# Where six weight casts stand in ScalarE's order at the start of a two-mixer decoder layer

## The chip, the cores and the metric

One core of a Trainium2 chip runs one launch of the whole layer. The metric is the device time of that launch in microseconds (us), the median of three runs.

## The reference

One post-norm layer on 1024 tokens of width 1024, batch 1, all in float32:

```
h    = layer_norm(x)
proj = h @ w_in                                   # 1024 x 11296
u, b_gate, c_gate, z_a, z_s, xbc, dt_raw, g_a, g_s = split(proj)
y_a  = (silu(z_a) * b_gate * conv3(c_gate * u)) @ w_a_out
xs, bs, cs = split(silu(conv4(xbc) + bias))
dt   = softplus(dt_raw + dt_bias)
y_s  = ssd_chunked(xs, dt, -exp(a_log), bs, cs) + xs * d_skip     # chunks of 128 tokens
y_s  = grouped_rmsnorm(y_s * silu(z_s)) @ w_s_out
out  = (sigmoid(g_a) * y_a + sigmoid(g_s) * y_s) @ w_o
h    = layer_norm(alpha * h + out)
```

## The kernel before, in words

Matrix products run in three float32r passes: a weight is split into a head (a cast, tile `whip`) and a rest (the weight minus its head, tile `wlop`), the activations likewise, and head x head, head x rest and rest x head are added up in PSUM. Heads of weights are cast by ScalarE (`prep_hi`), rests are subtracted by VectorE (`prep_lo`).

The input projection takes 44 pairs of column tiles. Each pair runs as seven Strassen-Winograd products of 512-token, 512-row pieces (`PROD`: which weight combination meets which activation combination). A product of a pair is an item: 12 matmuls of 128x128 by 128x512. The first three pairs (`EARLY = 3`) are worked through together, product by product in the order 1, 2, 3, 6, 5, 7, 4, so items 0 to 20 are "early" and item 21 (`START`) is where the steady part begins. Items 0 to 2 are product 1 (`a11` with `b11`, into `pU`), items 3 to 5 product 2 (`a12` with `b21`), items 6 to 8 product 3, whose weight `s4` GpSimd makes from `a12` and other sums.

Product 1 and 2 need only the first 512 tokens; product 3 needs the second 512 (`b22`), and products 6, 5, 7, 4 need sums over quarters of the normalised activations (`quarter_sums`, tiles `t`). The start of the program is therefore:

- the first half of the layer norm (`x0` to `x3`), eight transposed tiles, their evacuation by ScalarE (`evac`, `hf0...`), and the heads and rests of `b11` and `b21` by VectorE;
- statistics and norms of the second half (`factors(4)`, `norm(4)`, ..., `norm(6)`; `x4` to `x7`), on VectorE and ScalarE;
- items 0 to 5, then `dt_project(0)` (the projection `dps0` of the step sizes), then `second_half()`: 32 transposes in three PSUM banks, their evacuations, and between them the heads of items 6, 7 and 8.

For this early part a scheduler orders each engine's instructions by what it expects to be ready, except for instructions issued through `q(engine, f)`: these stand on their engine in the order in which the code issues them. The layer norm, the evacuations and the transposes of the first half, and GpSimd's sums go through `q`; matmuls, rests of weights and the additions from PSUM (`oa`) don't. GpSimd's `s4` of pair 0 also waits for the norm of `x7` on VectorE, and GpSimd's eight later sums stand behind it. From item 21 on the order is the written one.

In the code, all heads of the early pairs, items 0 to 20, go through `q` on ScalarE (item 0's is cast by VectorE). The loop over the items that asks for them is written behind the norms of the second half:

```
        if eng is None and kind == "p" and i < EARLY:
            q(S, lambda: S.activation(flat(hi), src, AF.Copy))
```

Of the kernel before, what the change touches and what calls it, by code (L numbers as in the profile page):

```python
# [45 lines left out]
def trunk_kernel(ctx: ExitStack, tc: tile.TileContext, x, w_in, w_dt, w_a, w_s, w_o, par, con,  # L46
# [60 lines left out]
    def flat(t):  # L107
        return t.rearrange("p k f -> p (k f)")
# [76 lines left out]
    EARLY = 3  # L185
# [19 lines left out]
    items += [("s", g, j) for g, j in s_order]  # L205
    item_at = {it: n for n, it in enumerate(items)}
    LA, LF = 3, 5

    raws, s1s, ops = {}, {}, {}

# [6 lines left out]
    def fetch(n):  # L217

        if n >= len(items) or items[n][:2] in raws or items[n] in raws:
            return  # L220
        kind, i, j = items[n]
        if kind == "p":
            for w in ("a11", "a12", "a21", "a22"):
                fetch_block(i, w)
        else:
            r = rawt(f"raw_{kind}{i}_{j}")
            SP.dma_start(r, w_a[i, :, j * HALF:(j + 1) * HALF] if kind == "a" else
                         w_s[4 * i + j // 2, :, j % 2 * HALF:(j % 2 + 1) * HALF])
            raws[items[n]] = r

    def combine(p):

        if p in s1s:
            return
        r = raws["p", p]
        s1, s2 = (est.tile([P, HALF], F32, name=f"e{n}_{p}") if p < 2 and n == "s1" else
                  r["a11"] if p < 2 else ap.tile([P, HALF], F32, tag=n, name=f"{n}_{p}") for n in ("s1", "s2"))
        fs = [lambda: Gp.tensor_tensor(s1, r["a21"], r["a22"], ALU.add),  # L238
              lambda: Gp.tensor_tensor(s2, s1, r["a11"], ALU.subtract),
              lambda: Gp.tensor_tensor(r["a21"], r["a11"], r["a21"], ALU.subtract)]  # L240
        if p < 2:
            fs = [fs[0], fs[2], fs[1]]
        for f in fs:
            q(Gp, f) if p < EARLY else f()
        s1s[p] = {"s1": s1, "s3": r["a21"], "s2": s2}

    def combine_last(p):

        if "s4" in s1s[p]:
            return  # L250
        a12 = raws["p", p]["a12"]
        f = lambda: Gp.tensor_tensor(a12, a12, s1s[p]["s2"], ALU.subtract)  # L252
        if p < EARLY:
            ins = q(Gp, f)
            if p == 0:
                tc.add_manual_dep(ins.ins, normed[0].name,
                                  mybir.DependencyInfo(mybir.DependencyClass.Sync, mybir.DependencyReason.DATA), reason="later")
        else:
            f()
        s1s[p]["s4"] = a12  # L260

    def source(n):
        kind, i, j = items[n]
        if kind != "p":
            return raws[items[n]]
        which = PROD[j][0]
        if which[0] == "s":
            combine(i)
            if which == "s4":
                combine_last(i)  # L270
            return s1s[i][which]
        return raws["p", i][which]
# [3 lines left out]
    def prep_hi(n, eng=None):  # L276

        if n >= len(items) or n in his:
            return
        fetch(n)  # L280
        src = source(n)
        kind, i, j = items[n]
        hi = his[n] = ap.tile([P, 4, P], F32R, tag="whi", name=f"whi{kind}{i}_{j}", bufs=LA + 1)
        if eng is None and kind == "p" and i < EARLY:
            q(S, lambda: S.activation(flat(hi), src, AF.Copy))
        elif eng is None:
            S.activation(flat(hi), src, AF.Copy)  # L287
        else:
            eng.tensor_copy(flat(hi), src)
# [10 lines left out]
    def prep(n, eng=None):  # L300
        prep_hi(n, eng)
        return prep_lo(n)
# [43 lines left out]
    def q(eng, f):  # L346

        if eng in last:
            with tc.issue_after(last[eng].ins):
                ins = f()  # L350
        else:
            ins = f()
        last[eng] = ins
        return ins
# [85 lines left out]
    def second_half():  # L440
        order = (4, 5, 6, 7, 0, 1, 2, 3)
        trs = {k: bank(("c4", "tr", "st")[i % 3], f"tr1{k}") for i, k in enumerate(order)}
        for k in order:
            for s in (4, 5, 7, 6):
                PE.transpose(trs[k][:, s % 4 * P:(s % 4 + 1) * P], xs[s][:, k * P:(k + 1) * P], ident)
            evac(1, k, trs[k])
            if k in (5, 7, 1):
                prep_hi(2 * EARLY + (5, 7, 1).index(k))
# [31 lines left out]
    def dt_turn():  # L480
        trd = bank("tr", "trd")
        trd3 = trd.rearrange("p (c h) -> p c h", c=NCH)
        for c in range(NCH):
            PE.transpose(trd3[:, c, :], dT[c // 4][:2 * H, c % 4 * P:(c % 4 + 1) * P], ident[:2 * H, :2 * H])
        w4.append(cv("w4").rearrange("p (i h c) -> p i h c", i=4, h=H))
        v = w4[0][:, 0]
        S.activation(v, trd3[:, :, 0:H].rearrange("p c h -> p h c"), AF.Copy)
        V.tensor_tensor(v, v, trd3[:, :, H:].rearrange("p c h -> p h c"), ALU.add)
        V.tensor_tensor(v, v, db_t.unsqueeze(2).to_broadcast([P, H, NCH]), ALU.add)
# [406 lines left out]
    def load_gy(j):  # L896
        M[j] = place(SG[j], f"sg{j}")
        SP.dma_start(M[j], sgs_d[j])
        gy[j] = otile(f"yg{j}", j % 2 if j < KT - 1 else 0)
        SP.dma_start(gy[j], yag_d[j])  # L900
# [159 lines left out]
    for n, it in enumerate(items):  # L1060
        if it[0] == "p" and it[2] == 1:
            first_of[n] = it[1]
    START = 7 * EARLY
    dt_work, first_cv = None, -1
    for n, (kind, i, j) in enumerate(items):
        now[0] = n
        for k in range(n, n + LF + 1):
            fetch(k)
        if n >= START and n + 2 in first_of:
            combine(first_of[n + 2])  # L1070
        if n >= START and n - 2 in first_of:
            combine_last(first_of[n - 2])
        if n < START:
            for k in range(n, min(n + LA + 1, 2 * EARLY if n < 2 * EARLY else START + LA)):
                prep_hi(k)
                if k < n + LA:
                    prep_lo(k)
        else:
            prep_hi(n + LA)
            prep_lo(n + LA - 1)  # L1080
        hi, lo = ops.pop(n)
        ops[n] = None
        if kind == "p":
# [6 lines left out]
            if n == 4 * EARLY + 1:  # L1090
                dt_project(1)
                dt_turn()
            if n == START - 1:
                est.release()
# [10 lines left out]
        if n in gy_at:  # L1105
            load_gy(gy_at[n])
        if n == START - 1:
            dt_work = dt_steps()
# [150 lines left out]
```

## Time and profile before

| | |
|---|---|
| median of three runs | 1420.25 us (1419.54, 1420.25, 1424.09) |
| the profiled execution | 1420.99 us, span of the core 1418.8 us |
| TensorE busy | 1383.5 us, 98% of the span |
| VectorE, ScalarE, GpSimd busy | 975.8, 701.4, 485.5 us |

The profile is of one execution. Its span runs from the first to the last instruction of the core; its own time holds 2.2 us besides. Times inside the profile are counted from the span's start. Items 0 to 20, on which the change acts, lie in the first 110 us or so.

### The profile page before, as it was taken

To read this page: it belongs to the slowest core of one execution; us is meant where nothing else is said; L and a number is where in the kernel's file an instruction comes from. 1 tells how busy PE (TensorE), PEld (TensorE's weight loads), DVE (VectorE), ACT (ScalarE), POOL (GpSimd) and SP (SyncE) were. 2 spreads that over 40 slices of the span, in tenths; PEclk is the share of its full clock that TensorE was granted. 3 is DMA by queue.
4 is the path that set the end of the run, shared out by engine and by line. 5 is a ranking of instruction groups with operands and counts; after the bars stand their busy time and mean duration, and the time that the engine had idled before them with its cause. 6 is when DMAs were issued, how large, how long until landed. Compare 5 with 4: busy or idle time off the path is not lost. (4 is left out here: it accounts for less than half of the span.)

```text
span 1418.8 us, 18394 instructions
## 1 busy us (share of the span) xinstructions
PE 1383.5 (98%) x6532; PEld 1111.4 (78%) x6532; DVE 975.8 (69%) x1422; ACT 701.4 (49%) x1228; POOL 485.5 (34%) x367
## 2 busy tenths in 40 slices
PE   6899999999999999999999999999999999999997
PEld 4677887888887888887888888888878888888786
DVE  7776878787779778688878686767464463224764
ACT  4465566555466655566566565555452231113421
POOL 1312124444425454334444343434230000000496
PEclk9899999999999999999999999999999999999999
DMA  6012354554444555444555654554547663223322
GB/s 237 15 67 83 118 134 130 126 182 127 145 125 132 144 165 151 131 130 123 156 156 182 134 153 127 153 126 127 186 163 267 232 228 133 90 82 118 127 89 89
DMA packets 166459, 198.09 MB, mean 140 GB/s; under 512 B 10688, under 2 KB 116064, under 8 KB 166368
## 3 DMA queue, kind: packets, MB, share of 16 engines
q1 hardware_dynamic: 158160, 167.14, 40.5%
q10 hardware_dynamic: 8208, 29.79, 5.3%
q8 instruction: 51, 0.84, 0.2%
q14 instruction: 40, 0.33, 0.1%
HBM read 146.28 MB, written 50.61 MB: 139 GB/s over the span
## 5 line engine op out<-in xcount | busy, mean ns | idle before, releaser
L105 DVE TENSOR_TENSOR wlop<-raw_a,whip 128x512 fp32r<-128x512 f32 x210 | 186.0, 886 | 158.7 <-ACT whip L287 63.9
L1015 PE MATMUL p<-b,whip 128*128 128x512 f32 x352 | 145.1, 412 | 7.2 <-DVE oa L1024 4.4
L1015 PE MATMUL pU<-t,whip 128*128 128x512 f32 x352 | 145.1, 413 | 0.0
L1015 PE MATMUL p<-t,whip 128*128 128x512 f32 x352 | 142.0, 403 | 0.0
L1016 PE MATMUL p<-b,whip 128*128 128x512 f32 x352 | 141.5, 402 | 0.0
L1017 PE MATMUL p<-b,wlop 128*128 128x512 f32 x352 | 140.8, 400 | 0.0
L1016 PE MATMUL pU<-t,whip 128*128 128x512 f32 x352 | 139.3, 396 | 0.0
L1017 PE MATMUL p<-t,wlop 128*128 128x512 f32 x352 | 139.1, 395 | 0.0
L1016 PE MATMUL p<-t,whip 128*128 128x512 f32 x352 | 139.1, 395 | 0.0
L1017 PE MATMUL pU<-t,wlop 128*128 128x512 f32 x352 | 139.0, 395 | 0.0
L675 POOL TENSOR_TENSOR xw<-xd,dte_t 128x256 f32<-128x256 f32 x56 | 46.9, 838 | 260.8 <-DVE xd L661 260.8
L287 ACT ACTIVATE whip<-raw_a 128x512 fp32r<-128x512 f32 x205 | 124.4, 621 | 22.4 <-issue 10.5
L940 POOL TENSOR_TENSOR res<-res,ag 128x1024 f32<-128x1024 f32 x8 | 19.7, 2462 | 276.1 <-ACT res L939 271.2
L238 POOL TENSOR_TENSOR s<-raw_a,raw_a 128x512 f32<-128x512 f32 x42 | 69.2, 1648 | 97.9 <-DVE wlop L105 85.8
L859 PE MATMUL p_ws<-y,whis 128*128 128x512 f32 x256 | 100.9, 394 | 0.0
L858 PE MATMUL p_ws<-y,whis 128*128 128x512 f32 x256 | 100.8, 394 | 0.0
L860 PE MATMUL p_ws<-y,wlos 128*128 128x512 f32 x256 | 100.7, 393 | 0.0
L105 DVE TENSOR_TENSOR wlos<-raw_s,whis 128x512 fp32r<-128x512 f32 x32 | 22.2, 693 | 113.0 <-PE p_ws L860 89.2
L252 POOL TENSOR_TENSOR raw_a<-raw_a,s 128x512 f32<-128x512 f32 x42 | 67.5, 1607 | 90.3 <-issue 78.8
L105 DVE TENSOR_TENSOR wlop<-s,whip 128x512 fp32r<-128x512 f32 x84 | 80.3, 966 | 13.4 <-PE p L1017 8.5
L1015 PEld LDWEIGHTS p<-b,whip 128*128 128x128 f32 x352 | 67.4, 192 | 23.7 <-issue 4.8
L641 ACT ACTIVATE em<-em,cum_t 128x128 f32<-128x128 f32 x256 | 81.3, 390 | 6.5 <-ACT ob L585 3.6
(224 smaller groups left out, 3345.7 us busy)
## 6 DMA issues: line engine op xcount, KB each, us to landing
raw_a<-in_w_in_dram SPq DMA_DIRECT2D x168, 256.0 KB, 3.9
em<-cum_d SPq DMA_DIRECT2D x64, 256.0 KB, 7.0
xg_d<-cv ACTq DMA_DIRECT2D x16, 512.0 KB, 6.4
xT<-xg_d SPq DMA_DIRECT2D x32, 256.0 KB, 4.6
z<-zs_d SPq DMA_DIRECT2D x32, 256.0 KB, 2.9
gat_d<-y SPq DMA_DIRECT2D x32, 256.0 KB, 2.9
gt<-gat_d SPq DMA_DIRECT2D x16, 512.0 KB, 6.7
raw_s<-in_w_s_dram SPq DMA_DIRECT2D x32, 256.0 KB, 4.1
```

The costliest lines, as they stand in the source:

```text
L105: return eng.tensor_tensor(lo, full, hi.bitcast(F32), ALU.subtract)
L238: fs = [lambda: Gp.tensor_tensor(s1, r["a21"], r["a22"], ALU.add), lambda: Gp.tensor_tensor(s2, s1, r["a11"], ALU.subtract), lambda: Gp.te ...
L252: f = lambda: Gp.tensor_tensor(a12, a12, s1s[p]["s2"], ALU.subtract)
L287: S.activation(flat(hi), src, AF.Copy)
L641: S.activation(em[:, h, :], em[:, h, :], AF.Relu, bias=cum_t[:, 8 * g + 4 * i + h, c:c + 1], scale=-1.0)
L675: Gp.tensor_tensor(xw, XD[n, i], dte_t[:, hs, c].unsqueeze(2).to_broadcast([P, HG, HD]), ALU.mult)
L858: PE.matmul(ps, lhsT=hi[:, k, :], rhs=u[:, 0, :], start=start, stop=False)
L859: PE.matmul(ps, lhsT=hi[:, k, :], rhs=u[:, 1, :], start=False, stop=False)
L860: PE.matmul(ps, lhsT=lo[:, k, :], rhs=u[:, 0, :], start=False, stop=stop)
L1015: PE.matmul(ps, lhsT=hi[:, k, :], rhs=u[:, 0, :], start=first, stop=False, skip_group_check=True)
L1016: PE.matmul(ps, lhsT=hi[:, k, :], rhs=u[:, 1, :], start=False, stop=False, skip_group_check=True)
L1017: PE.matmul(ps, lhsT=lo[:, k, :], rhs=u[:, 0, :], start=False, stop=(k == 3), skip_group_check=True)
```

## The change

The heads of items 0 to 5 no longer go through `q`; those of items 6 to 20 still do. `START` is only moved up, which puts every later line of the changed kernel one line further down.

```diff
     LA, LF = 3, 5
+    START = 7 * EARLY
...
-        if eng is None and kind == "p" and i < EARLY:
+        if eng is None and 2 * EARLY <= n < START:
             q(S, lambda: S.activation(flat(hi), src, AF.Copy))
         elif eng is None:
             S.activation(flat(hi), src, AF.Copy)
...
-    START = 7 * EARLY
```

The order of SyncE and GpSimd is the same in both kernels; on TensorE, VectorE and ScalarE it differs in the early part alone.

**ScalarE.** `whip1_2` is the head of pair 1 for product 2, `hf00` the first evacuation, `oa1` the evacuation of `pU1`. Before, all five heads stand behind the norm of `x6`, the last of the second half:

```order
L370 ACTIVATE ln1_6_350<-mv_t_118,eps_t_116 128x2
L384 ACTIVATE x6_172<-x6_172,nb_t_120,rs_t_119 128x1024
L285 ACTIVATE whip1_1_360<-e1_a11_157 128x512
L285 ACTIVATE whip2_1_364<-raw2_a11_159 128x512
L285 ACTIVATE whip0_2_368<-e0_a12_161 128x512
L285 ACTIVATE whip1_2_387<-e1_a12_163 128x512
L285 ACTIVATE whip2_2_406<-raw2_a12_165 128x512
L1031 ACTIVATE oa1_390<-pU1_389 128x512
L393 ACTIVATE hf10_497<-tr14_485,par_t_115 128x512
```

Now three of them stand behind the norm of `x2`, the last of the first half, in front of all evacuations:

```order
L385 ACTIVATE x2_145<-x2_145,nb_t_120,rs_t_119 128x1024
L288 ACTIVATE whip1_1_360<-e1_a11_157 128x512
L288 ACTIVATE whip2_1_364<-raw2_a11_159 128x512
L288 ACTIVATE whip0_2_368<-e0_a12_161 128x512
L394 ACTIVATE hf00_286<-tr00_202,par_t_115 128x512
```

The other two stand behind the eight evacuations of the first half, still in front of the second half's norms, and the evacuations `oa1` and `oa2` have come forward with them.

**VectorE.** Before, the rests of items 1 to 4 stand behind the norm of `x7`, here in its last rows:

```order
L376 SCALAR_TENSOR_TENSOR rs_t_119<-ln1_6_350,rs_t_119 128x2
L377 SCALAR_TENSOR_TENSOR nb_t_120<-mv_t_118,rs_t_119 128x2
L382 TENSOR_SCALAR x7_174<-x7_174,rs_t_119,nb_t_120 128x1024
L105 TENSOR_TENSOR wlop1_1_362<-e1_a11_157,whip1_1_360 128x512
L105 TENSOR_TENSOR wlop2_1_366<-raw2_a11_159,whip2_1_364 128x512
L105 TENSOR_TENSOR wlop0_2_385<-e0_a12_161,whip0_2_368 128x512
L105 TENSOR_TENSOR wlop1_2_404<-e1_a12_163,whip1_2_387 128x512
L397 CAST b22_0_499<-hf10_497 128x512
```

Now that norm has the last addition of product 2 (`oa2`) in front of it and no rest behind it:

```order
L1025 TENSOR_TENSOR oa2_409<-p2_2_453,oa2_409 128x512
L374 RECIPROCAL rs_t_119<-ln1_6_350 128x2
L375 TENSOR_TENSOR ln1_6_350<-rs_t_119 128x2
L376 TENSOR_TENSOR ln1_6_350<-ln1_6_350,ln0_6_349 128x2
L377 SCALAR_TENSOR_TENSOR rs_t_119<-ln1_6_350,rs_t_119 128x2
L378 SCALAR_TENSOR_TENSOR nb_t_120<-mv_t_118,rs_t_119 128x2
L383 TENSOR_SCALAR x7_174<-x7_174,rs_t_119,nb_t_120 128x1024
L398 CAST b22_0_499<-hf10_497 128x512
```

The rests `wlop1_1` and `wlop2_1` have moved in front of the first head of `b11`, and `wlop0_2`, `wlop1_2`, `wlop2_2` and the additions `oa0`, `oa1`, `oa2` in among `b21` and the statistics of `x4` to `x7`; in front of the norm of `x7` stand eight more instructions of 128x512 than before.

**TensorE.** Before, the projection `dps0` and twelve transposes of the second half (`tr14` to `tr16`) stand between item 0 and items 1 and 2:

```order
L475 MATMUL dps0_467<-b21_3_323,wdt_186 64x512
L445 MATMUL tr14_485<-con_t_114,x4_168 128x128
L445 MATMUL tr15_486<-con_t_114,x4_168 128x128
L445 MATMUL tr16_487<-con_t_114,x4_168 128x128
...
L445 MATMUL tr14_485<-con_t_114,x6_172 128x128
L445 MATMUL tr15_486<-con_t_114,x6_172 128x128
L445 MATMUL tr16_487<-con_t_114,x6_172 128x128
L1015 MATMUL pU1_389<-b11_0_288,whip1_1_360 128x512
L1016 MATMUL pU1_389<-b11_0_288,whip1_1_360 128x512
```

Now items 1 to 5 come first, interleaved with item 0, and `dps0` and all 32 transposes follow behind the last matmul of item 5:

```order
L1016 MATMUL p2_2_453<-b21_3_323,whip2_2_406 128x512
L1017 MATMUL p2_2_453<-b21_3_323,whip2_2_406 128x512
L1018 MATMUL p2_2_453<-b21_3_323,wlop2_2_423 128x512
L475 MATMUL dps0_467<-b11_0_288,wdt_186 64x512
L476 MATMUL dps0_467<-b11_0_288,wdt_186 64x512
```

From the first matmul of item 8 (`p3_2`), which is product 3's first in both kernels, TensorE's order is the same but for a few neighbours in products 6 and 5.

## Rows read from the trace of the kernel before

**Rows 1.** The page, part 1: busy time, share of the span and instructions of TensorE.

```profile
PE 1383.5 (98%) x6532; PEld 1111.4 (78%) x6532; DVE 975.8 (69%) x1422; ACT 701.4 (49%) x1228; POOL 485.5 (34%) x367
```

**Rows 2.** What TensorE (PE) waited for in the first 110 us, by the instruction that ended the wait: total, times, longest.

```profile
PE p L1015 <- DVE oa L1024: 4.4, 1, 4.4
PE tr L445 <- ACT x L384: 4.1, 2, 3.9
```

**Rows 3.** TensorE in order of time: start and length in us, then line, operation, tiles, shape, how many, and in brackets the idle time before it and what ended it. `pU<-b` is product 1 of a pair, `p<-b` product 2 (until 58.45) and then product 3, `dps` the projection of the step sizes, `tr` a transpose, `pU<-t` product 6.

```profile
18.16 0.51 PE L1015 MATMUL pU<-b,whip 128*128 128x512 f32 x1 [0.57 <-DVE b L397]
...
28.33 0.44 PE L475 MATMUL dps<-b,wdt 128*64 128x512 f32 x1 [0.28 <-DVE b L105]
32.69 0.90 PE L445 MATMUL tr<-con_t,x 128*128 128x128 f32 x3 [3.92 <-ACT x L384]
...
43.45 0.39 PE L1015 MATMUL p<-b,whip 128*128 128x512 f32 x1
...
48.81 0.40 PE L1017 MATMUL p<-b,wlop 128*128 128x512 f32 x1
53.62 0.76 PE L1015 MATMUL p<-b,whip 128*128 128x512 f32 x1 [4.41 <-DVE oa L1024]
...
58.45 0.63 PE L1017 MATMUL p<-b,wlop 128*128 128x512 f32 x1
...
62.84 0.50 PE L1015 MATMUL p<-b,whip 128*128 128x512 f32 x1 [0.53 <-ACT whip L285]
...
71.55 0.40 PE L1015 MATMUL pU<-t,whip 128*128 128x512 f32 x1
...
81.22 0.45 PE L475 MATMUL dps<-t,wdt 128*64 128x512 f32 x1 [0.63 <-DVE t L105]
```

**Rows 4.** ScalarE (ACT) in order of time, same columns. `x<-x` is a norm, `hf<-tr` an evacuation of a transpose, `whip` a head; the row at 62.16 is the head of pair 2 in product 3.

```profile
14.52 1.24 ACT L384 ACTIVATE x<-x,nb_t,rs_t 128x1024 f32<-128x1024 f32 x1 [2.98 <-DVE nb_t L377]
16.87 5.47 ACT L393 ACTIVATE hf<-tr,par_t 128x512 f32<-128x512 f32 x8 [1.10 <-PE tr L420]
...
34.97 1.24 ACT L384 ACTIVATE x<-x,nb_t,rs_t 128x1024 f32<-128x1024 f32 x1 [1.02 <-DVE nb_t L377]
36.12 0.61 ACT L285 ACTIVATE whip<-e_a 128x512 fp32r<-128x512 f32 x1
36.64 0.61 ACT L285 ACTIVATE whip<-raw_a 128x512 fp32r<-128x512 f32 x1
...
62.16 0.63 ACT L285 ACTIVATE whip<-raw_a 128x512 fp32r<-128x512 f32 x1
```

**Rows 5.** VectorE (DVE) in order of time, same columns. `wlop` is a rest of a weight, `b<-hf` the head (CAST) or the rest of a piece of the activations, `oa<-p,oa` an addition of a product from PSUM, `t<-hf,hf` the first quarter sum; the RECIPROCAL at 33.99 and the row at 34.97 belong to the second half's last norm.

```profile
15.71 0.69 DVE L105 TENSOR_TENSOR wlop<-e_a,whip 128x512 fp32r<-128x512 f32 x1
17.68 0.43 DVE L397 CAST b<-hf 128x512 fp32r<-128x512 f32 x1 [1.28 <-ACT hf L393]
...
18.83 0.95 DVE L397 CAST b<-hf 128x512 fp32r<-128x512 f32 x1
...
33.99 0.17 DVE L373 RECIPROCAL rs_t<-ln 128x2 f32<-128x2 f32 x1 [0.18 <-ACT ln L370]
...
34.97 0.81 DVE L382 TENSOR_SCALAR x<-x,rs_t,nb_t 128x1024 f32<-128x1024 f32 x1
...
37.38 0.69 DVE L105 TENSOR_TENSOR wlop<-raw_a,whip 128x512 fp32r<-128x512 f32 x1
37.98 0.68 DVE L105 TENSOR_TENSOR wlop<-e_a,whip 128x512 fp32r<-128x512 f32 x1
...
42.67 0.61 DVE L397 CAST b<-hf 128x512 fp32r<-128x512 f32 x1 [0.83 <-ACT hf L393]
...
44.91 1.77 DVE L105 TENSOR_TENSOR wlop<-raw_a,whip 128x512 fp32r<-128x512 f32 x1
...
52.80 0.68 DVE L1024 TENSOR_TENSOR oa<-p,oa 128x512 f32<-128x512 f32 x1
...
62.12 0.68 DVE L456 TENSOR_TENSOR t<-hf,hf 128x512 f32<-128x512 f32 x1
```

**Rows 6.** GpSimd (POOL) in order of time, same columns. The rows from 38.74 on are the first, the sixth and the last of nine that make `s4` and the other weight sums of the early pairs.

```profile
16.54 1.27 POOL L239 TENSOR_TENSOR e_a<-es,e_a 128x512 f32<-128x512 f32 x1 [2.27 <-DVE wlop L105]
...
38.74 1.29 POOL L252 TENSOR_TENSOR e_a<-e_a,e_a 128x512 f32<-128x512 f32 x1 [19.24 <-DVE wlop L105]
...
46.09 1.73 POOL L238 TENSOR_TENSOR s<-raw_a,raw_a 128x512 f32<-128x512 f32 x1
...
50.89 1.44 POOL L252 TENSOR_TENSOR raw_a<-raw_a,s 128x512 f32<-128x512 f32 x1
```

**Rows 7.** Busy time of the engines in two stretches, then the granted clock of TensorE (1.00 is 2.4 GHz), the DMA engines' share and GB/s.

```profile
31.80:38.60 6.80, 4.56 (x16) 3.48 (x17) 5.36 (x15) 5.48 (x8) 0.00 (x0) 0.50 0.01 2
...
52.30:59.10 6.80, 5.48 (x14) 4.24 (x15) 2.37 (x4) 0.00 (x0) 0.03 (x1) 0.50 0.08 29
```

**Rows 8.** The DMA issues of the first 75 us, from one view of them: issue of two pieces of weights in order of time (start, length).

```profile
8.25 0.99 SPq L215 DMA_DIRECT2D e_a<-in_w_in_dram  x2
```

**Rows 9.** The same DMA issues by tile: how many, KB each, median us from issue to landing.

```profile
e_a<-in_w_in_dram SPq DMA_DIRECT2D x8, 256.0 KB, 6.7
```

**Rows 10.** What TensorE waited for from 85 us to the end, same columns as in rows 2.

```profile
PE p_wo L1153 <- DVE wo L105: 2.4, 2, 1.8
PE tr L649 <- DVE xd L661: 2.2, 1, 2.2
```

## The prediction

> **What bounds the kernel now.** First the page's busy shares: TensorE is busy for 98% of the span [rows 1], so a gain has to come out of a place where it waits or runs slowly. Then its waits over the first 110 us: two stand out, 3.9 us for a norm on ScalarE and 4.4 us for an addition on VectorE [rows 2]. TensorE's rows in order of time place them. Item 0 starts at 18.16, `dps0` is through at 28.77, and the queue then stands until 32.69 for the norm of `x4`; items 1 to 4 run until 49.2, and item 5 waits until 53.62 [rows 3], because it writes the bank of item 3, whose addition VectorE reaches only at 52.80 [rows 5]. Third, the granted clock: behind each of the two waits it is 0.50, that is 1.2 GHz, for 6.8 us [rows 7]. A matmul comes every 0.233 us at full clock (24 from 43.45 to 48.81) and every 0.44 us at half (12 from 53.62 to 58.45) [rows 3].
>
> What ends the stretch stands in two more queues. Product 3 starts at 62.84, when the head of item 8 is cast [rows 3, 4]; that head reads the last of GpSimd's nine sums, done at 52.33 [rows 6], but ScalarE reaches it only at 62.16, behind evacuations of transposes that stand behind item 5 on TensorE. And the quarter sums begin on VectorE at 62.12 [rows 5]; they end TensorE's last wait of the early part, at 81.22 [rows 3]. Later it waits little [rows 10].
>
> **The change, step by step.** Nothing is added or removed; 5 heads, 5 rests and 3 additions move, with 60 matmuls behind them.
>
> *Three heads before the evacuations.* ScalarE has the norm of `x2` done at 15.76. A head takes 0.52 us (36.12 to 36.64) [rows 4], so three end at 17.32; the first evacuation began at 16.87, so it comes 0.45 us later. Their data are there: the last pair of issues at 8.25 to 9.24 plus 6.7 us gives 15.9 at the latest [rows 8, 9], and the second of these is needed only later.
>
> *Two rests before the first head of `b11`.* A rest costs 0.60 us alone (37.38 to 37.98) and up to 1.77 us while GpSimd works (44.91) [rows 5]. VectorE is free at 16.31, and GpSimd runs one sum from 16.54 to 17.81 [rows 6]. No row has a rest beside that sum; the nearest, a head beside GpSimd's next work, took 0.95 us instead of 0.43 [rows 5]. Below, ScalarE's 0.45 us decides; above, two rests of 1.7 us make the head 2.1 us late. As one GpSimd sum can meet only one of them, I take 0.9 us: the head at 18.6, item 0 at 19.1.
>
> The Trainium skill, page "SBUF — State Buffer", section "Who interferes with whom", says that a VectorE instruction with two SBUF inputs and a GpSimd instruction that reads SBUF can't share a port pair: the second waits until the first is through. By it the second rest would wait for 17.81 and the first head start at 18.4, so the sum below would gain 0.2 us; the rows between 44 and 52 us agree, with one VectorE instruction to each GpSimd sum.
>
> *Items 0 to 5 in one piece.* TensorE now has 72 matmuls behind each other. From 19.1, with 0.3 us of waits for the first rest of `b11`, they take 72 x 0.233 = 16.8 us, until 36.2. Both waits and most of the half clock between go, but not what stood behind them: `dps0` (16 x 0.233 = 3.7 us) follows until 39.9.
>
> *The norm of `x7`.* This is what the change makes late. Three more rests and three additions of 0.60 us now stand in front of it, 3.6 us besides the 0.9, less about 0.1 us that they fill of waits between dependent small operations. The last addition needs item 5, through at 36.2; VectorE gets there at about 37.5, so it doesn't wait. The norm ended at 35.78 [rows 5] and ends at 40.2. GpSimd's sums may start only behind it: 40.2 instead of 38.74.
>
> *GpSimd's nine sums.* They took 13.6 us (38.74 to 52.33), 1.29 us each alone and up to 1.73 beside VectorE [rows 6]. TensorE's transposes follow `dps0` and the norm of `x6` at about 41, so `b22` reaches VectorE near 42.7 as before [rows 5], and as before about seven of its instructions fall among the sums, one to each. I keep 13.6: done at 53.8. All nine alone would be 11.6, all beside VectorE 15.6.
>
> *Product 3.* ScalarE now waits for nothing else: head 0.63 us, TensorE at 54.5 instead of 62.84, 8.3 us earlier. But it has idled since the transposes, about 8 us with little between, so I let the clock come back as it did behind the second wait: half clock until 5.5 us after the restart, 13 matmuls, 13 x 0.2 = 2.6 us lost. The 36 matmuls end at 54.5 + 8.4 + 2.6 = 65.5, where product 6 began at 71.55 [rows 3]: 6.0 us earlier. With no half clock it is 8.6, with all 36 at half clock 1.4.
>
> The Trainium skill, page "TensorE: Matmul & The Clock Gate", section "Why this matters for your kernels", warns of pauses between bursts of matmuls, since they cost the full clock. By it one longer pause is no cure for two shorter ones; the half clock in rows 7 agrees, and the 2.6 us are already in the sum.
>
> *The quarter sums.* At 53.8 VectorE has left one head of `b22` (0.45 us) and three rests (1.8), so the first quarter sum starts at 56.1 instead of 62.12: 6.0 us earlier. TensorE's last wait behind them moves from 81.22 to 75.2.
>
> Both paths give 6.0 us. From item 21 on every queue is as written and moves along. So 1420.99 - 6.0 = 1415.0 us for the profiled execution; its time lies 0.7 us above the median of three, so 1414.3 us.
>
> **The rivals.** About 0.3%, 4.3 us, is what a measurement of this kernel can tell from no change.
>
> *GpSimd's queue ends later still.* All nine sums at 1.73 us cost 2.0 us, both rests beside GpSimd 1.2 us more, and the gain is 2.8: 1417.5 us. For it speaks that VectorE has no free time among the sums; against it that the same seven instructions met them before.
>
> *More is kept.* With the sums nearer 1.29 us (2 us less), 0.45 instead of 0.9, and the clock back at once, both paths gain 8.5: 1411.8 us. Against it speaks the long pause before product 3.
>
> *The gain is given back later*, where a transfer or VectorE sets the pace: 1420 us. Against it: the two largest waits from 85 us on are 4.6 us together in 1330 us [rows 10].
>
> *Slower.* VectorE's queue now holds the addition of item 5 in front of the norm of `x7`, so whatever makes TensorE late there makes the whole second half late. If the clock fell in the short wait before item 0 and stayed at half, 72 matmuls at 0.43 would end at 50.3, the norm at 52.8 (0.7 for the addition, 1.8 from the reciprocal at 33.99 to 35.78 [rows 5]), GpSimd at 66.4, the quarter sums would start at 68.7, and the kernel take 6.5 us more: 1426.8 us. It decides from the point where item 5 ends after about 43.7. Against it: behind the wait of 0.57 us before item 0 the first matmul lasts 0.51 us now, at half clock 0.76 (at 53.62) [rows 3].
>
> That the change doesn't do what it says is excluded by the order shown above.
>
> **How the numbers follow.** Forecast 0.66 (own range 1412.6 to 1416), GpSimd later 0.16, more kept 0.09, given back 0.05, slower 0.04. The time is the forecast's. The range goes from more kept, 1411.0, to past GpSimd later, 1418.5; what lies outside is given back, slower and the edges, under 2 in 10. Faster by over 0.3% (below 1416.0): 0.66 + 0.09 = 0.75; slower 0.04; the rest, 0.21, the same.
>
> **What the profile would show.** Right: no wait over 1 us on TensorE between item 0 and the transposes; the norm of `x7` ending near 40, GpSimd's nine sums from there to near 54; product 3 starting within 1 us of their end, with ScalarE's head between; between 16 and 100 us a granted clock of 0.50 behind that pause alone; the first quarter sum near 56. Wrong: the norm of `x7` after 42, VectorE waiting for item 5 in front of it, GpSimd's sums over 15 us, another stretch at half clock there, or a new wait beyond 100 us of more than 1 us.

## The result and the profile after

The changed kernel takes 1414.34 us (median of six runs, 1414.18 to 1416.05) against 1422.12 us for the kernel before beside it (1419.52 to 1424.33): 0.995 of its time, with a 95% interval of 0.9933 to 0.9966. The profiled execution took 1414.21 us, its span is 1412.3 us, 6.5 us less than before.

TensorE's busy time hardly moves, and its large waits of the early part are others than before [rows 1, 2]:

```profile
PE 1378.9 (98%) x6532; PEld 1110.9 (79%) x6532; DVE 976.6 (69%) x1422; ACT 701.9 (50%) x1228; POOL 485.2 (34%) x367
```

TensorE's waits of the first 110 us (total, times, longest):

```profile
PE p L1016 <- ACT whip L286: 4.8, 1, 4.8
PE tr L446 <- ACT hf L394: 2.9, 3, 1.7
...
PE pU L1016 <- DVE b L398: 1.8, 1, 1.8
```

The 3.9 us for a norm and the 4.4 us for the addition are gone; a wait of 1.8 us ahead of item 0 and one of 4.8 us ahead of product 3 have come. In order of time on TensorE [answers rows 3] (here and below, rows of the changed kernel to be read against the group of that number before):

```profile
19.31 0.50 PE L1016 MATMUL pU<-b,whip 128*128 128x512 f32 x1 [1.78 <-DVE b L398]
...
22.78 0.63 PE L1016 MATMUL pU<-b,whip 128*128 128x512 f32 x1
23.20 0.63 PE L1018 MATMUL pU<-b,wlop 128*128 128x512 f32 x1
...
38.44 0.40 PE L1018 MATMUL p<-b,wlop 128*128 128x512 f32 x1
...
55.21 0.79 PE L1016 MATMUL p<-b,whip 128*128 128x512 f32 x1 [4.83 <-ACT whip L286]
...
65.43 0.39 PE L1016 MATMUL pU<-t,whip 128*128 128x512 f32 x1
...
75.69 0.45 PE L476 MATMUL dps<-t,wdt 128*64 128x512 f32 x1 [0.64 <-DVE t L105]
```

Items 0 to 5 run in one piece but for a wait of 0.64 us at 20.45: the first matmul starts at 19.31, the last at 38.44. But around 22.78 and 23.20 a matmul comes only every 0.43 us. The granted clock of that stretch, of the stretch that was at half clock before, and of the pause ahead of product 3 (busy times, then the clock, as in [rows 7]):

```profile
21.90:24.90 3.00, 3.00 (x8) 2.31 (x7) 2.93 (x6) 0.80 (x2) 0.00 (x0) 0.50 0.73 244
31.80:38.60 6.80, 6.80 (x31) 5.46 (x30) 6.59 (x18) 2.67 (x3) 0.00 (x0) 1.00 0.00 1
52.30:59.10 6.80, 3.89 (x9) 3.07 (x10) 6.76 (x10) 3.77 (x7) 2.20 (x2) 0.51 0.22 77
```

The other queues of the early part: ScalarE [answers rows 4],

```profile
15.70 0.62 ACT L288 ACTIVATE whip<-e_a 128x512 fp32r<-128x512 f32 x1
...
17.26 1.42 ACT L394 ACTIVATE hf<-tr,par_t 128x512 f32<-128x512 f32 x2
...
54.53 0.63 ACT L286 ACTIVATE whip<-raw_a 128x512 fp32r<-128x512 f32 x1 [4.18 <-POOL raw_a L253]
```

VectorE [answers rows 5]: the two rests of items 1 and 2, the first head of `b11`, two rests of later items that wait, the last addition of product 2, the norm of `x7`, the first quarter sum, and a rest that waits for product 3,

```profile
16.96 1.76 DVE L105 TENSOR_TENSOR wlop<-raw_a,whip 128x512 fp32r<-128x512 f32 x1
18.64 0.61 DVE L398 CAST b<-hf 128x512 fp32r<-128x512 f32 x1
...
26.04 0.69 DVE L105 TENSOR_TENSOR wlop<-e_a,whip 128x512 fp32r<-128x512 f32 x1 [0.45 <-PE pU L1018]
...
30.52 0.69 DVE L105 TENSOR_TENSOR wlop<-raw_a,whip 128x512 fp32r<-128x512 f32 x1 [0.90 <-issue]
...
38.87 0.69 DVE L1025 TENSOR_TENSOR oa<-p,oa 128x512 f32<-128x512 f32 x1
...
40.46 0.81 DVE L383 TENSOR_SCALAR x<-x,rs_t,nb_t 128x1024 f32<-128x1024 f32 x1
...
57.11 0.68 DVE L457 TENSOR_TENSOR t<-hf,hf 128x512 f32<-128x512 f32 x1
...
60.50 0.69 DVE L105 TENSOR_TENSOR wlop<-e_a,whip 128x512 fp32r<-128x512 f32 x1 [0.30 <-PE p L1018]
```

GpSimd [answers rows 6]; the last row is its first addition behind the early part, 111.83 before, and serves below as the mark of where the early part ends:

```profile
16.57 1.60 POOL L240 TENSOR_TENSOR e_a<-es,e_a 128x512 f32<-128x512 f32 x1 [2.27 <-DVE wlop L105]
...
41.40 1.29 POOL L253 TENSOR_TENSOR e_a<-e_a,e_a 128x512 f32<-128x512 f32 x1 [21.55 <-issue]
...
53.06 1.44 POOL L253 TENSOR_TENSOR raw_a<-raw_a,s 128x512 f32<-128x512 f32 x1
...
106.29 1.28 POOL L253 TENSOR_TENSOR raw_a<-raw_a,s 128x512 f32<-128x512 f32 x1 [19.66 <-issue]
```

The mark is 5.54 us earlier than before. From there all rows stay 5.5 to 5.6 us earlier until about 220 us, and then 6.4. Those 0.8 us are no work of the change: before, the matmuls behind the 2.19 us wait for `xd` [rows 10] ran at half clock from 216 us on; in this execution the same wait stands there without it. Run 12, the kernel before without that stretch, has a span of 1417.8 us, 1.0 us less. Of the stretch from 210 to 225 us, before and after (PE alone):

```profile
210.00:225.00 15.00, 12.81 (x63) 0.89 0.51 180
```

```profile
210.00:225.00 15.00, 14.14 (x72) 1.00 0.47 102
```

So the change itself took some 5.5 us off this execution's early part, and nearly all the rest of the 6.5 us is clock. The medians are 7.8 us apart, but the clock has a part in that too. Among the executions of the kernel before beside runs 9 to 12, those with a mean granted clock of 0.992 took 1419.3 to 1419.6 us, those with 0.985 to 0.987 1423.2 to 1424.4; the changed kernel's with 0.992 took 1414.1 to 1414.3. At the same clock the gain is some 5 us.

### The profile page after: what moved, and what is told of

Same layout as the page of the kernel before. It is cut to its first block, busy times and chain, and to the rows that moved or that the text cites. A ratio compares the mean times of both kernels' runs of the same rounds, so it can differ in the third digit from the quotient of the medians.

```text
span 1412.3 us, 18391 instructions
## 1 busy us (share of the span) xinstructions
PE 1378.9 (98%) x6532; PEld 1110.9 (79%) x6532; DVE 976.6 (69%) x1422; ACT 701.9 (50%) x1228; POOL 485.2 (34%) x367
## 5 line engine op out<-in xcount | busy, mean ns | idle before, releaser
L288 ACT ACTIVATE whis<-raw_s 128x512 fp32r<-128x512 f32 x32 | 20.3, 633 | 129.6 <-PE p_ws L860 109.0
```

## The experiments

Theory: TensorE's wait at item 5 and the idle time ahead of it are gone because items 1 to 5 run during the second half's norms; the end of the early part is then set by VectorE's queue (norm of `x7`, heads and rests of `b22` beside GpSimd's nine sums, quarter sums). Rivals: the wait at item 5's bank was all of it; GpSimd's nine sums set the end; the half clock ahead of product 3 does.

One table first, from the traces. "Mark" is GpSimd's first addition behind the early part, "`x7`" the start of its norm on VectorE, "sum" the first quarter sum, "p3" the start of product 3, "half clock" the stretches between 19 and 76 us in which TensorE's granted clock is 0.50. The medians belong to three sessions, in which the kernel before took 1420.27 (1 to 4), 1422.46 (5 to 8) and 1422.64 us (9 to 12); the first two rows are those of the sections above. The 95% interval of a ratio to the kernel before reaches 0.0012 to 0.0017 to either side, some 2 us, so differences of one or two microseconds between the variants are read from the marks, one profiled execution each, and are not settled by the medians.

| | mark | `x7` | sum | p3 | half clock | median |
|---|---|---|---|---|---|---|
| before | 111.83 | 34.97 | 62.12 | 62.84 | 31.8-38.6, 52.3-59.1 | 1422.12 |
| after | 106.29 | 40.46 | 57.11 | 55.21 | 21.5-24.9, 52.2-59.0 | 1414.34 |
| 1 before, other bank | 107.67 | 34.89 | 58.24 | 58.70 | 31.6-41.8 | 1416.22 |
| 2 items 1, 2 free only | 104.44 | 36.22 | 54.83 | 53.90 | 21.1-24.5, 38.1-41.6 | 1413.34 |
| 3 fill | 105.41 | 38.74 | 55.48 | 54.25 | none | 1415.28 |
| 4 `s3` late | 105.82 | 40.34 | 57.01 | 53.70 | 20.4-23.8, 51.1-58.0 | 1415.03 |
| 5 `b22` heads on ScalarE | 107.14 | 40.30 | 55.30 | 55.54 | 20.8-24.2, 48.1-61.8 | 1417.22 |
| 6 sums not held | 104.64 | 45.67 | 55.83 | 54.94 | 36.0-39.5 | 1413.76 |
| 7 two rests later | 105.62 | 39.03 | 55.41 | 54.12 | 48.6-58.8 | 1415.05 |
| 8 = 4 and 5 | 103.44 | 38.82 | 53.85 | 52.41 | 46.6-56.8 | 1413.79 |
| 9 after, again | 104.36 | 38.89 | 55.55 | 53.65 | 49.8-56.6 | 1414.22 |
| 10 = 2, 4 and 5 | 102.77 | 35.84 | 52.09 | 52.34 | 20.7-24.1, 37.8-41.2 | 1411.72 |
| 11 = 10, other bank | 105.19 | 35.92 | 53.78 | 54.67 | 21.6-25.0, 38.6-42.1, 55.7-59.1 | 1413.95 |
| 12 before, again | 111.67 | 35.41 | 61.96 | 62.68 | 30.6-40.9, 54.5-57.9 | 1420.02 |

**1. The bank alone.** Item 5's result to another bank of PSUM, in the kernel before.

```diff
-    EBANK = {(0, 1): "U", (1, 1): "yy", (2, 1): "yy", (0, 2): "cx", (1, 2): "U", (2, 2): "cx",
+    EBANK = {(0, 1): "U", (1, 1): "yy", (2, 1): "yy", (0, 2): "cx", (1, 2): "U", (2, 2): "st",
```

> The kernel before, with one thing changed: item 5's result goes to another bank of PSUM, so that it does not wait for VectorE's addition of item 3's result. ScalarE's order stays that of the kernel before: the heads of items 3 to 5 still stand behind the second half's norms. Theory A (the order of ScalarE is what held the early part): TensorE still does items 1 to 5 behind the transposes and only the 4.4 us wait at item 5 and the half clock that came behind it go, so the gain is smaller than the whole change's: 1 to 4 us against the kernel before, and the first quarter sum lies between the changed kernel's 57.11 us and the 62.12 us of before. Theory B (the change gained by this bank's wait alone): the run comes to the changed kernel's time within 1 us, some 5 us under the kernel before, and product 3 starts at 55 to 57.5 us.

Measured: 0.9968 of the time before (0.9955 to 0.9982); the mark 4.16 us earlier than before. No wait for the addition is left. Both theories missed their numbers, the first by 0.2 us, the second by more: product 3 starts 3.5 us later than in the changed kernel. So taking the wait at item 5 away, with the half clock that stood behind it, is worth 4.2 us by itself, more than half of what the change gives (5.5 us here, 7.5 us in run 9), and not all of it. The edit isn't quite clean: "st" is also one of the three banks that the transposes of the second half use, so four of them go behind item 5, and ScalarE waits for them:

```profile
54.82 1.45 ACT L393 ACTIVATE hf<-tr,par_t 128x512 f32<-128x512 f32 x2 [8.96 <-PE tr L445]
```

**2. Only items 1 and 2 free.**

```diff
-        if eng is None and 2 * EARLY <= n < START:
+        if eng is None and EARLY <= n < START:
```

> The changed kernel, with only the heads of items 1 and 2 free in ScalarE's order; those of items 3 to 5 go back behind the first norm of the second half. Theory A (what counts is that TensorE has something to do during the second half's norms, and VectorE's queue then sets the end): VectorE meets only two rests ahead of its norms, so the norm of x7 ends some 4 us earlier than the changed kernel's 41.27 us, while TensorE does three items behind the transposes; the two effects nearly cancel: product 3 starts at 53.5 to 56 us and the time is within 1.5 us of the changed kernel's. Theory B (all five items must be out of the way): items 3 to 5 behind the transposes bring back the 4.4 us wait at item 5's bank, and at least 3 us of the change's gain is gone.

Measured: 0.995 (0.9938 to 0.9963), mark 1.85 us before that of the changed kernel, with a stretch at half clock from 21 us in both. Theory A holds: the norm of `x7` starts 4.2 us earlier, and TensorE has three items left for the time after the transposes, so only 1.39 us of waiting stand ahead of product 3 instead of 4.83 (the wait for item 3's addition is back, but at 0.88 us). By the marks the first two heads alone gave more than all five; the ratios, 0.995 for both, don't tell the two kernels apart. What the other three cost was no wait of TensorE: their rests and additions stand in front of the norm of `x7` on VectorE.

**3. TensorE kept busy ahead of product 3.** 18 matmuls behind the last transposes.

```diff
-                PE.transpose(trs[k][:, s % 4 * P:(s % 4 + 1) * P], xs[s][:, k * P:(k + 1) * P], ident)
+                tr = PE.transpose(trs[k][:, s % 4 * P:(s % 4 + 1) * P], xs[s][:, k * P:(k + 1) * P], ident)
...
+        u = B["b11", 0]
+        ps = bank("cx", "fill")
+        with tc.issue_after(tr.ins):
+            for i in range(18):
+                PE.matmul(ps, lhsT=u[:, 0, :P], rhs=u[:, 0, :], start=True, stop=True)
```

> The changed kernel with 18 more matmuls of 512 columns on a block of b that lies ready, put behind the second half's last transposes, in the pause ahead of product 3; their result is used nowhere. They take away most of the pause of 4.83 us and so may take away the half clock behind it (52.19 to 59.0 us, 3.8 us of it under matmuls). Theory A (VectorE's quarter sums and GpSimd's chain set the end of the early part, the half clock is hidden): product 3's matmuls are faster, the time changes by less than 0.6 us. Theory B (the half clock is on the path): 1.7 to 2 us faster than the changed kernel, half of 3.8 us.

Measured: 0.9966 (0.9954 to 0.9979). The clock stays at 1.00 from 19 to 80 us:

```profile
19.00:80.00 61.00, 52.95 (x234) 1.00 0.11 38
```

TensorE reaches product 6 at 62.76, in run 9 at 63.49. But then it waits for quarter sums, from ScalarE and from VectorE:

```profile
PE pU L1021 <- ACT t L468: 1.5, 1, 1.5
PE pU L1022 <- DVE t L105: 1.2, 1, 1.2
```

Run 9 is the execution of the changed kernel that like this one has no half clock at 21.5 us. There the same waits are 0.63 and 0.64 us, the first quarter sum starts at the same time (55.55, here 55.48), and the mark is 1.05 us earlier than here. So full clock ahead of product 3 gave nothing back: what TensorE gained it spent waiting for VectorE's sums. That is Theory A's mechanism, though not its number. Of the microsecond lost, product 3's later start (0.60 us), its faster run (1.33 us less) and the longer waits (1.52 us more) make up 0.8. Why TensorE had no other work for these waits is open; the order of some matmuls in products 6 and 5 changed with the edit.

**4. One sum less in GpSimd's chain.** The third pair's `s3` is kept back until its `s4` is through.

```diff
+        elif p < EARLY:
+            last_sum[p] = fs.pop()
...
+        if p == EARLY - 1:
+            for f in last_sum.values():
+                q(Gp, f)
```

> The changed kernel with GpSimd's sum s3 of the third pair moved behind its s4 sum, so that the chain of GpSimd's sums ahead of product 3's heads is shorter by one, about 1.6 us; all work stays. Theory A (VectorE's quarter sums, behind the heads and rests of b22, set the end of the early part): product 3 starts about 1.5 us earlier than 55.21 us, but the first quarter sum stays at 57.1 us within 0.5 us, and the time falls by 0 to 0.5 us. Theory B (GpSimd's nine sums alone set it): both fall by 1.5 us, and so does the time.

Measured: 0.9961 (0.9948 to 0.9975). Product 3 starts 1.51 us earlier, the first quarter sum 0.10, the mark 0.47: Theory A, in all three, by the marks; the ratio is no better than the changed kernel's. GpSimd's sums set the start of product 3, but hardly the end of the early part: 0.37 of the 0.47 us come behind the first quarter sum, where VectorE's wait of 0.30 us for product 3 (60.50 above) is gone.

**5. `b22`'s heads on ScalarE.**

```diff
-            q(V, lambda: V.tensor_copy(u[:, 0, :], full))
+            if name == "b22":
+                q(S, lambda: S.activation(u[:, 0, :], full, AF.Copy))
+            else:
+                q(V, lambda: V.tensor_copy(u[:, 0, :], full))
```

> The changed kernel with the four heads of b22 cast by ScalarE instead of VectorE, so that VectorE's queue ahead of the quarter sums loses four operations which beside GpSimd's sums take about 1.5 us each. Theory A (VectorE's queue sets the first quarter sum, 57.11 us, and with it the end of the early part at 75.69 us): the first quarter sum is 1.5 to 2.5 us earlier, product 3's start stays within 0.5 us of 55.21 us, and the time falls by 0.5 to 1.5 us. Theory B (the start of product 3 sets the end): no change within 0.4 us.

Measured: 0.9962 (0.9948 to 0.9976). The first quarter sum came 1.81 us earlier, as Theory A has it, but the mark is 0.85 us later, which neither expected. The half clock explains it: here it lasts from 48.1 to 61.8 us (first row), and VectorE, no longer the last, waits for product 3 (second fence):

```profile
48.10:61.80 13.70, 9.14 (x27) 0.50 0.11 38
```

```profile
61.92 0.69 DVE L105 TENSOR_TENSOR wlop<-e_a,whip 128x512 fp32r<-128x512 f32 x1 [2.14 <-PE p L1021]
```

How much of the half clock ahead of product 3 is on the path, VectorE's wait for product 3 tells: nothing in run 9 (6.8 us of half clock, until 56.6), 0.30 us in the first profile of the changed kernel (6.8 us, until 59.0), 1.30 us in run 7 (10.2 us, until 58.8), 2.14 us here. Whether the edit made it longer (the transposes now come in fours with waits of 0.4 to 1.2 us between) or this execution alone has it isn't settled; run 8, with the same heads on ScalarE, has 10.2 us, and so has run 7 without them.

**6. GpSimd's sums not held behind the norm of `x7`.**

```diff
-            if p == 0:
-                tc.add_manual_dep(ins.ins, normed[0].name,
-                                  mybir.DependencyInfo(mybir.DependencyClass.Sync, mybir.DependencyReason.DATA), reason="later")
```

> The changed kernel without the order that holds GpSimd's nine sums behind the norm of x7. They then start at some 27 us, beside VectorE's rests and norms. Theory A (GpSimd's sums and VectorE's operations stretch each other): the norm of x7 moves from 41.27 us to 45 to 48 us, GpSimd's nine sums start 14 us earlier but end only 0 to 3 us earlier than 54.50 us, and the time stays within 2 us of the changed kernel's. Theory B (the chain from the norm of x7 through the nine sums is the bound and nothing stretches): the sums end 10 us or more earlier and the time falls by 5 us or more.

Measured: 0.994 (0.9926 to 0.9955). First and last of the nine sums, and the norm of `x7`:

```profile
26.21 1.62 POOL L253 TENSOR_TENSOR e_a<-e_a,e_a 128x512 f32<-128x512 f32 x1 [6.46 <-ACT oa L1029]
...
38.59 1.28 POOL L253 TENSOR_TENSOR raw_a<-raw_a,s 128x512 f32<-128x512 f32 x1
```

```profile
45.67 0.81 DVE L380 TENSOR_SCALAR x<-x,rs_t,nb_t 128x1024 f32<-128x1024 f32 x1
```

Each theory has one half right. The sums end at 39.87, 14.6 us earlier than in the first profile and 13.1 than in run 9 (Theory B), yet the mark is within 0.3 us of run 9's, which has no half clock at 21.5 us either (Theory A). Against run 9 the norm of `x7` starts 6.8 us later, and from there to the first quarter sum it takes 6.5 us less (10.16 instead of 16.66). So GpSimd's end is not the bound. That it is the time which VectorE spends beside GpSimd, wherever it lies, fits both numbers and is not shown beyond that.

**7. The rests of items 1 and 2 later.**

```diff
+        if n in (1, 2):
+            with tc.issue_after(first_rest[1].ins):
+                return sub_split(flat(lo), source(n), flat(his[n]), V)
...
-            q(V, lambda: sub_split(u[:, 1, :], full, u[:, 0, :], V))
+            done = q(V, lambda: sub_split(u[:, 1, :], full, u[:, 0, :], V))
+            first_rest.append(done)
```

> The changed kernel with VectorE's rests of items 1 and 2 put behind its head and rest of the first two blocks of b, so that item 0 does not wait for a rest that ran beside a GpSimd sum. Theory A (the wait of 1.78 us ahead of item 0 is what the stretch at half clock from 21.5 to 24.9 us came behind): item 0 starts 0.5 to 1 us earlier than 19.31 us, the stretch is gone or shorter, items 1 to 5 end about 2 us earlier, the norm of x7 ends about 1 us earlier, and the time falls by 0.5 to 1 us. Theory B (the stretch comes of what TensorE did before 17 us, not of this wait): the stretch stays and the time changes by less than 0.5 us.

Measured: 0.9957 (0.9941 to 0.9973). Item 0 starts at 18.41 behind a wait of 0.94 us, the clock doesn't fall at 21.5 us, the mark is 0.67 us earlier: all that Theory A wanted. It is not shown all the same, since run 9 has the same clock there without the edit, and a mark 1.26 us earlier still. The difference lies behind the first quarter sum, where VectorE waits for product 3, which ran at half clock until 58.8:

```profile
59.80 0.69 DVE L105 TENSOR_TENSOR wlop<-e_a,whip 128x512 fp32r<-128x512 f32 x1 [1.30 <-PE p L1023]
```

**8. Edits 4 and 5 together.**

> The changed kernel with both edits at once: the s3 sum of the third pair behind its s4 sum on GpSimd, and b22's heads on ScalarE. Theory A (two chains end near each other, GpSimd's sums into product 3 and VectorE's queue into the quarter sums, and only shortening both pays in full): product 3 starts about 1.5 us earlier, the first quarter sum 2 us earlier, and the time falls by 1.5 to 2.5 us, more than either edit alone. Theory B (one of them alone binds): the time is that of the better of the two single edits, within 0.4 us.

Measured: 0.9941 (0.9927 to 0.9955). Against run 9, which like it has full clock from 19 to 46 us: first quarter sum 1.70 us earlier, product 3 1.24, mark 0.92. More than edit 4 alone brought (0.47), less than Theory A's 1.5; between the sum and the mark 0.8 us went. 0.6 of them are one rest, which run 9 has in front of the first quarter sum (54.95) and this run behind it (55.05). VectorE doesn't wait for product 3 here, though half clock lasts 10.2 us.

**9. The changed kernel again**, with no edit.

> The changed kernel itself, profiled a second time. The question is the stretch at half clock from 21.5 to 24.9 us, which stood in the profiles of four kernels of this family behind a wait of 1.8 to 1.9 us ahead of item 0 and was missing in two others behind the same wait of 1.92 us. Theory A (it comes by chance, not by the kernel): this profile either shows it again, and the first GpSimd addition behind the early part starts at 106.3 us as before, or does not, and it starts 1.4 to 1.8 us earlier; with either, the stretch of half clock just ahead of product 3 stays and the early part's chain is the same. Theory B (the wait makes it): the stretch is there and the addition starts at 106.3 us within 0.2 us.

Measured: 1414.22 us as median, 0.9945 (0.9932 to 0.9959); the profiled execution has a span of 1409.5 us. Theory A, with a mark 1.93 us earlier where 1.4 to 1.8 were expected: the wait ahead of item 0 is 1.91 us, the clock stays up behind it,

```profile
21.90:24.90 3.00, 3.00 (x14) 2.41 (x14) 2.93 (x6) 1.46 (x4) 0.00 (x0) 1.00 0.69 228
```

14 matmuls instead of 8 run in those 3 us, no rest on VectorE waits between 20 and 32 us (the first profile has the two above, 1.35 us), and the later rows up to the first quarter sum are 1.56 us earlier:

```profile
38.89 0.81 DVE L383 TENSOR_SCALAR x<-x,rs_t,nb_t 128x1024 f32<-128x1024 f32 x1
...
43.23 0.76 DVE L398 CAST b<-hf 128x512 fp32r<-128x512 f32 x1 [3.52 <-ACT hf L394]
...
55.55 0.68 DVE L457 TENSOR_TENSOR t<-hf,hf 128x512 f32<-128x512 f32 x1
```

The norm of `x7`, the first sum on GpSimd (41.40 and 39.84), product 3 and the first quarter sum all move by the same 1.56 or 1.57 us: that is one chain, and lateness of TensorE in items 1 to 5 passes through it in full. The mark moves by 1.93: the other 0.37 us come with the wait for product 3 at 60.50, which the first profile has and this one hasn't. From the first head of `b22` at 43.23, behind its wait of 3.52 us for the evacuations, VectorE waits for nothing until 81.00: in this execution its queue alone sets the pace of that stretch.

**10. Edits 2, 4 and 5 together.**

> Three edits to the changed kernel at once: only the heads of items 1 and 2 free in ScalarE's order, the third pair's s3 sum behind its s4 sum on GpSimd, and b22's heads cast by ScalarE. Theory A (the end of the early part is set by VectorE's queue and GpSimd's sums, and each edit shortens one of them): the first quarter sum starts at 50.5 to 53 us and the first GpSimd addition behind the early part 1 to 3 us earlier than the 104.44 us it had with the first edit alone, so the time is 1 to 3 us lower than with that edit. Theory B (TensorE takes over as the bound, by a pause of some 3 us ahead of product 3 and half clock behind it): the addition stays at 104.4 us or later.

Measured: 1411.72 us, 0.9927 (0.9914 to 0.994), beside 1414.22 us for run 9 in the same session; span 1408.0 us. The mark is 1.67 us earlier than with edit 2 alone and 3.52 us earlier than the changed kernel's, and all three executions have a stretch at half clock from 21 us. Theory A. TensorE finds items to do until the transposes and waits only 0.67 us ahead of product 3:

```profile
52.34 0.50 PE L1026 MATMUL p<-b,whip 128*128 128x512 f32 x1 [0.67 <-ACT whip L293]
```

It is the fastest of the kernels here, 2.5 us or 0.2% below the changed kernel beside it; its interval still overlaps that of run 9, and those of runs 6 and 8.

**11. Run 10 with the other bank for item 5.**

> The three edits of the run before in this list and, with them, another bank of PSUM for item 5's result, so that TensorE does item 5 without waiting for VectorE's addition of item 3's result and has its pause elsewhere. Theory A (the pause's place matters only through the clock: the bank's wait is hidden beside GpSimd's sums): the first GpSimd addition behind the early part is within 0.5 us of the run without this edit. Theory B (the wait at item 5's bank costs by itself, as it did in the kernel before): 1 us earlier or more.

Measured: 0.9943 (0.9929 to 0.9956), the mark 2.42 us later than in run 10, which neither theory had. As in run 1, the bank belongs to the transposes too: four of them now stand behind item 5, and ScalarE's evacuation, which VectorE's rests of `b22` wait for, comes later:

```profile
49.48 0.78 ACT L401 ACTIVATE hf<-tr,par_t 128x512 f32<-128x512 f32 x1 [7.58 <-PE tr L456]
```

In run 10 the same evacuation starts at 41.73. The first quarter sum comes 1.69 us later than in run 10, and behind it VectorE waits 1.66 us for product 3, which run 10 doesn't have. In run 10 TensorE had no wait for the bank left to remove.

**12. The kernel before again**, with no edit.

> The kernel before itself, profiled a second time, to see what of its early part comes again. If the early part is the same in each execution, the wait for item 3's addition ahead of item 5 is again 4.4 us, half clock stands behind it, and the first GpSimd addition behind the early part starts at 111.8 us within 0.3 us; if half clock comes and goes by chance there, it starts up to 2 us earlier or later.

Measured: the time of the kernel before (0.9995, 0.9981 to 1.0009), the mark 0.16 us off. The clock differed all the same: half clock until 40.9 instead of 38.6 us; the wait at item 5 shrank by 0.45 us, and a shorter stretch at half clock behind it made up the rest:

```profile
54.42 0.67 PE L1015 MATMUL p<-b,whip 128*128 128x512 f32 x1 [3.96 <-DVE oa L1024]
```

The kernel before takes up such a stretch, the changed one doesn't, between items 1 to 5 and the norm of `x7`.

## Why the prediction was right

- *Heads before the evacuations.* Predicted to end at 17.32; the first evacuation starts at 17.26.
- *Rests before `b11`.* Predicted 18.6 for its first head, found 18.64, with the mechanism assumed: one rest alone, one at 1.76 us beside GpSimd's sum. That sum was itself stretched to 1.60 us, so a lock that holds back VectorE alone (the reading I made of the Trainium skill, page "SBUF — State Buffer", section "Who interferes with whom", at 18.4) is 0.24 us too short.
- *Items 0 to 5.* This step failed in part. I let 72 matmuls run at full clock from 19.1 to 36.2; they ran from 19.31 to 38.7 in one profile and from 19.31 to 37.1 in the other (run 9). The term that I left out is a stretch at half clock behind the wait of 1.8 us, 1.6 us long in its effect; another such stretch was on my own list of signs of being wrong. I had seen that danger only as the rival "slower", in which the clock stays down for good, and had weighed it by the matmul right behind the wait, which is at full clock (0.50 us) here too; the fall came 2 us later. Without that stretch the step was right to 0.9 us.
- *Norm of `x7`.* Predicted end 40.2; 41.27 and 39.70. That TensorE's lateness comes through to this norm I had only for the addition of item 5; in the first profile it came by the two rests that wait 0.45 and 0.90 us, and both are gone in run 9. VectorE doesn't wait for item 5, as predicted, but with nothing to spare, where I had 1.3 us: item 5's last matmul is over at 38.84, the addition starts at 38.87.
- *GpSimd's nine sums.* Predicted 13.6 us, found 13.10 in both. *Product 3*: predicted 54.5, found 55.21 and 53.65, with ScalarE's head right behind the last sum. *Product 6*: predicted 65.5, found 65.43 and 63.49. The first hit is two errors that cancel: product 3 started 0.7 us late and lost 1.8 us to half clock instead of 2.6.
- *Two paths of equal length.* The sum made the path through product 3 as long as that through the quarter sums. In the first profile they nearly are: VectorE waits 0.30 us for product 3. But it is the second that counts: product 3 earlier by 1.5 us moves the mark by 0.47 (run 4), and full clock there doesn't move it forward (run 3). The half clock, 2.6 us in the sum, cost product 3 1.8 us in the first profile and 1.4 in run 9 (36 matmuls in 10.22 and 9.84 us instead of 8.4), and most or all of that was hidden; in runs 5 and 7 it was not.
- *Quarter sums and end.* Predicted 56.1 and 75.2; found 57.11 and 75.69, and in run 9 55.55 and 73.76. Predicted gain 6.0 us; the mark gives 5.54 and, in run 9, 7.47.
- *Given back later.* Nothing is: TensorE's waits from 85 us on are p_wo 2.4 and xd 2.2 us, as before.
- *The time.* 1414.3 forecast, 1414.34 measured; that it agrees to 0.1 us is luck. The sum gave 1415.0 us for the profiled execution, and it took 1414.21: the early part gave 0.5 us less than forecast, the clock at 216 us and the time outside the span together 1.2 us more. And the 0.7 us taken off for the median didn't hold: six runs of the kernel before have a median of 1422.12 us, which is above the profiled 1420.99 and not below it.

## What to carry to other kernels

Take an instruction out of a fixed order where TensorE would wait behind it, but count what then moves ahead of the next norm on VectorE: here, by the marks, the first two of five heads were worth 1.85 us more without the other three. When two queues end near each other, shorten both, for here either alone gave less than 0.5 us of the mark or a loss, both together 0.9, and both with the other three heads back in their place 3.5 (2.5 us of the median). And before a gain of one or two microseconds is put down to an edit, profile the same kernel twice: its own executions differ by as much, and one profile per variant doesn't settle such a difference.

## What the runs showed of the hardware

- Half clock comes and goes between executions of one program, behind the same wait. Behind 1.72 to 1.93 us of idle time ahead of item 0 the granted clock fell to 0.50 in the changed kernel's first profile and in runs 2, 4, 5, 10 and 11, and stayed at 1.00 in runs 6, 8 and 9 (1.91 and 1.92 us); behind the 2.19 us wait at about 215 us it was 0.50 in one profile of the kernel before and 1.00 in the other. The Trainium skill, page "TensorE: Matmul & The Clock Gate", section "Part 1: The HAM clock gate (the "warmup" mystery)", says that the point of change differs from run to run at the start of a kernel; the traces show it in the middle too.
- What such a stretch costs depends on what stands behind it: 1.6 us in the changed kernel at 21.5 us, by all rows up to the first quarter sum, nothing in the kernel before between 31 and 41 us, where the next wait and the stretch behind it took it up, 0.8 us at 216 us.
- A VectorE subtraction of 128x512 takes 0.68 us alone and 1.6 to 1.8 us beside GpSimd's additions, and those stretch from 1.27 to 1.6 or 1.7 us themselves. Moving the nine additions forward by 14 to 15 us (run 6) hardly moved the end, 0.3 us against run 9.
